# Weight differences of a Strassen output projection: own buffers and later stores for the second half, GpSimd alone for the first half

## The chip, the cores and the metric

The kernel runs on one core of one Trainium2 chip. The metric is the device time of one execution in microseconds (us); of several runs the median counts.

## What is computed

One decoder layer on 512 positions of width 2048, in float32. From the reference, cut to what matters here:

```python
mod = cond @ w_ada[l] + b_ada[l]
shift, scale, gate = jnp.split(mod, 3, axis=-1)
h = rms_norm(x, norm_g[l]) * (1.0 + scale[:, None, :]) + shift[:, None, :]
z = h @ w_in[l]
u_a, v_a, g_a, q_b, k_b, v_b, g_b, f_b = jnp.split(z, pts, axis=-1)
y_a = chunked_spatial_gating(gelu(u_a), gelu(v_a), ...) * silu(g_a)
y_b = forgetting_attention(q_b, k_b, v_b, f_b, b_f[l]) * silu(g_b)
y = jnp.concatenate([y_a, y_b], axis=-1) @ w_out[l]
x = x + gate[:, None, :] * y
return rms_norm(x, final_g)
```

## The kernel before, in words

Every float32 operand of a product is split into a high and a low part, and each product is made of three matmuls on TensorE: high by high, high by low, low by high. A weight tile is loaded into a ring of four buffers (tag `raw`), ScalarE writes the high part (`whi`, line 129) and VectorE the low part (`wlo`, line 130), both in rings of two (`w_tile`, lines 117 to 131). So a tile is split while TensorE works on the tile before it.

The stages follow each other in this order: the conditioning and `h`; the columns `u` and most of the gate of group A (tiles `st`); `v` of group A (`va`, 16 weight tiles); the rest of the gate (`ga`); then four passes of attention, each for four of the 16 heads: the columns `q`, `k`, `vb` and the gate `gb`; last the output projection.

Attention is woven into these products. After each weight tile `tick` (line 133) takes one entry of `slots` (attention, lines 468 to 565) and one of `fillers`. In a pass the scores are made first (lines 484 to 491), then `lse` (line 495) takes their logarithm, transposes it and splits it into `lt`, and eight small copies (line 507) carry `lt` into the rows of the `q` tiles that the second score products (lines 523 and 524, tile `t`) read.

The output projection is one level of a Strassen scheme. It needs four differences of the blocks of `w_out` for each half `u` of the columns. They are made early, beside other products, and kept in device memory (`tsum`): a step loads four blocks into one buffer, subtracts in place, and stores the result. For the first half this is `sum_step` (line 613), woven between the tiles of `va`, eight steps; the buffers are those of tags `vs` (even steps) and `pth`, `ptl` (odd steps), and the four subtractions of line 628 go in turn to GpSimd and VectorE. For the second half it is `sum_part` (line 635), sixteen pieces `ts{k}_{p}` half as wide, all on GpSimd (line 644); each piece takes one buffer of the ring `raw`, is loaded by lines 640 and 641 and stored by line 646. The fillers before them are the gate's steps (`gate_step`, line 594, and `gate_sum`, line 648), which use the ring `raw` too.

SP issues nearly all transfers, in one queue and in order. The order in each engine's queue is set by a scheduler when the program is built, from the order of the code, from priorities (weight tiles are put ahead) and from its own model of times; `tc.issue_after` holds an instruction behind another one.

The tile `wsp` holds the spatial weights of group A until `va` has been mixed; later `wide` (line 1000), scratch of the second output half, takes the same place.

Of the kernel before, what the change touches and what calls it, by code (L numbers as in the profile page):

```python
# [8 lines left out]
F32 = mybir.dt.float32  # L9
F32R = mybir.dt.float32r  # L10
BF16 = mybir.dt.bfloat16
AF = mybir.ActivationFunctionType
ALU = mybir.AluOpType
# [14 lines left out]
def trunk_kernel(  # L28
# [69 lines left out]

    newest = [None]
    newest_mm = [None]  # L100

    def load(dst, src, late=False):
        with ExitStack() as es:
            if queue:
                es.enter_context(tc.issue_after((newest[0] if late else queue[-1]).ins))
            newest[0] = nc.sync.dma_start(dst, src)
            if CHAIN[0]:
                queue.append(newest[0])

    hh = [None] * KB  # L110
    hl = [None] * KB
# [5 lines left out]
    def w_tile(segs, k0, nk, src=win_r, name="", pri=WPRI, loeng=None):  # L117
        n = sum(w for _, w in segs)
        with tc.high_priority(offset=pri):
            raw = wp.tile([P, nk, n], F32, tag="raw", name=f"raw_{name}", bufs=4)  # L120
            o = 0
            for c0, w in segs:
                (load if pri == 0 else nc.sync.dma_start)(
                    raw[:, :, o : o + w], src[:, k0 : k0 + nk, c0 : c0 + w]
                )
                o += w
            hi = wp.tile([P, nk, n], F32R, tag="whi", name=f"whi_{name}")
            lo = wp.tile([P, nk, n], F32R, tag="wlo", name=f"wlo_{name}")
            nc.scalar.activation(hi, raw, AF.Copy)  # L129
            (loeng or nc.vector).tensor_tensor(lo, raw, hi.bitcast(F32), ALU.subtract)  # L130
        return hi, lo
# [292 lines left out]

    fsplit = pb.tile([16, 2, S], F32R, name="fsplit", tag="fs")
    vs_ = []
    wsp = pb.tile([P, 8, 2, P], F32R, name="wsp", tag="wsp")
    OFF = [0, 512, 896, 1152]
    sgb = {}

# [182 lines left out]
    def sum_step(u, k):  # L613

        js = slice((k % 2) * 512, (k % 2) * 512 + 512)
        w = wout_r[:, :, u * 1024 : (u + 1) * 1024].rearrange("p k (s n) -> p k s n", s=2)
        if k % 2:
            a = [pb.tile([P, 2, 512], F32, tag=t, name=f"ts{t}{u}_{k}") for t in ("pth", "ptl")]
        else:
            o = pb.tile([P, 4, 512], F32, tag="vs", name=f"ts{u}_{k}")  # L620
            a = [o[:, 0:2, :], o[:, 2:4, :]]
        nc.sync.dma_start(a[0], w[:, 8 + k])
        nc.sync.dma_start(a[1], w[:, k])
        b11, b12, b21, b22 = (a[z // 2][:, z % 2, :] for z in range(4))
        for z, (dst, l, r) in enumerate((
            (b11, b12, b11), (b12, b12, b22), (b22, b22, b11), (b21, b21, b22),
        )):
            (nc.vector if z % 2 else nc.gpsimd).tensor_tensor(dst, l, r, ALU.subtract)
        if k % 2:
            nc.sync.dma_start(tsum[u][k // 2][:, 0:2, js], a[0])  # L630
            nc.sync.dma_start(tsum[u][k // 2][:, 2:4, js], a[1])
        else:
            nc.sync.dma_start(tsum[u][k // 2][:, :, js], o)

    def sum_part(u, k, p):

        c = slice(p * 256, p * 256 + 256)
        a = wp.tile([P, 4, 256], F32, tag="raw", name=f"ts{u}_{k}_{p}", bufs=4)
        w = wout_r[:, :, u * 1024 : (u + 1) * 1024].rearrange("p k (s n) -> p k s n", s=2)
        nc.sync.dma_start(a[:, 0:2, :], w[:, 8 + k, :, c])  # L640
        nc.sync.dma_start(a[:, 2:4, :], w[:, k, :, c])
        b11, b12, b21, b22 = (a[:, z, :] for z in range(4))
        for dst, l, r in ((b11, b12, b11), (b12, b12, b22), (b22, b22, b11), (b21, b21, b22)):
            nc.gpsimd.tensor_tensor(dst, l, r, ALU.subtract)  # L644
        o = (k % 2) * 512 + p * 256
        nc.sync.dma_start(tsum[u][k // 2][:, :, o : o + 256], a)

    def gate_sum(g):
        gsl = slice(2 * D + g * 512, 2 * D + (g + 1) * 512)
        bg = wp.tile([P, 512], F32, name=f"bg{g}", tag="raw", bufs=4)  # L650
        nc.sync.dma_start(bg, b_ada[:, gsl].broadcast_to([P, 512]))
        gp = bank("x", f"gp{g}")
        nc.tensor.matmul(gp, ones, gate[:, g, :], start=True, stop=True)
        nc.vector.tensor_tensor(gate[:, g, :], gp, bg, ALU.add)
# [4 lines left out]
    def spatial_weights():  # L659
        ws = wp.tile([P, 8, P], F32, tag="raw", name="ws", bufs=4)  # L660
        load(ws, w_s[0].rearrange("h t s -> t h s"), late=True)
        load(
            bias2.rearrange("p h t -> p (h t)"),
            b_s.rearrange("a h t -> a (h t)").broadcast_to([P, 8 * P]), late=True,
        )
        nc.gpsimd.affine_select(
            out=ws, in_=ws, pattern=[[0, 8], [-1, P]], compare_op=ALU.is_ge,
            fill=0.0, base=0, channel_multiplier=1,
        )
        for i in range(2):  # L670
            wt = bank("x", f"wsT{i}")
            for j in range(4):
                nc.tensor.transpose(wt[:, j * P : (j + 1) * P], ws[:, 4 * i + j, :], ident)
            wt32 = pb.tile([P, 512], F32, name=f"wt32_{i}", tag="p", bufs=2)
            nc.scalar.activation(wt32, wt, AF.Copy)
            split(
                wsp[:, 4 * i : 4 * i + 4, 0, :], wsp[:, 4 * i : 4 * i + 4, 1, :],
                wt32.rearrange("p (h t) -> p h t", t=P),
            )
            rp = bank("x", f"rsw{i}")  # L680
            nc.tensor.matmul(rp, ones, wt32, start=True, stop=True)
            for j in range(4):
                h = 4 * i + j
                nc.vector.scalar_tensor_tensor(
                    bias2[:, h, :], rp[:, j * P : (j + 1) * P], lngb[:, 8 + h : 9 + h],
                    bias2[:, h, :], ALU.mult, ALU.add,
                )
# [71 lines left out]
    def mix_head(h):  # L759
# [2 lines left out]
        js = slice(j * P, (j + 1) * P)  # L762
        mt = pb.tile([P, 512], F32, name=f"mt{h}", tag="p", bufs=2)
        b2 = bias2[:, h, :]
        w2 = wsp[:, h].rearrange("p a t -> p (a t)")
        for n in range(2):
            mx = bank("x", f"mix{h}_{n}")
            for i in range(2):
# [28 lines left out]
    vs_.append(pb.tile([P, NT, 4, P], F32R, name="vs", tag="vs"))  # L797
    v_group(0)
    heads_tiles()
    for g in range(4):  # L800
        for i in range(8):
            fillers.append(lambda g=g, i=i: gate_step(g, i))
            if g and i == 2:
                fillers.append(lambda g=g: gate_sum(g - 1))
    parts = [lambda k=k, p=p: sum_part(1, k, p) for k in range(8) for p in range(2)]
    fillers.extend(parts[:3] + [lambda: gate_sum(3)] + parts[3:])
    qk_group(0)
    g_group(0)
    for u in range(1, 4):
# [153 lines left out]
    def unit(u):  # L963
# [33 lines left out]
        X = [bank("x", f"woX{u}_{t}") for t in range(2)]  # L997
        product(X, "S2", w_sum(3, "p6"), True)
        if u:
            wide = pb.tile([P, 4, 512], F32, name="wide", tag="wsp")  # L1000
            u2, u3 = [wide[:, t, :] for t in range(2)], [wide[:, 2 + t, :] for t in range(2)]
        else:
            u2, u3 = tiles("u2", "yb", 8), tiles("u3", "yb", 8)
        evac(lambda t: nc.vector.tensor_tensor(u2[t], X[t], c1[t], ALU.add))
# [123 lines left out]
```

## Time and profile before

| | us |
|---|---|
| median of 3 runs (911.5 to 913.87) | 913.16 |
| the profiled execution: its own time | 910.78 |
| its span, first to last instruction | 909.1 |
| TensorE busy | 880.1 (97%) |
| VectorE busy | 603.9 (66%) |
| ScalarE busy | 445.4 (49%) |
| GpSimd busy | 405.9 (45%) |

The profile is of one execution. Matmuls are pipelined, so a busy TensorE can still lose time: the granted clock of a window says at what share of full speed it ran. A wait is named by what ended last before the instruction could start.

### The profile page before, as it was taken

The numbers are of one execution on the slowest core, as the hardware profiler recorded it, in microseconds if no ns is written. First come the engines' busy times: TensorE is split into PE (matmuls) and PEld (weight loads), VectorE is DVE, ScalarE is ACT, GpSimd is POOL, SyncE is SP. The second block draws the span as 40 slices with busy tenths as digits, with TensorE's granted clock in tenths as the row PEclk, the third lists the DMA queues.
The fourth block names the chain that finished last, engine by engine and source line by source line (L and its number), as shares of the span: only waits on it lengthen the run. The fifth ranks groups of instructions, "written<-read, shape, count | busy, mean of one in ns | idle before, by whom it ended". The sixth has DMA issues, their size and how long they took to land.

```text
span 909.1 us, 12698 instructions
## 1 busy us (share of the span) xinstructions
PE 880.1 (97%) x4408; PEld 744.3 (82%) x4408; DVE 603.9 (66%) x998; ACT 445.4 (49%) x775; POOL 405.9 (45%) x322
## 2 busy tenths in 40 slices
PE   6999999999999999999999999989999999999995
PEld 4888888887878997777889888978898888888884
DVE  4778888374547857454886554535655679996687
ACT  5663323452313234455666544645556657655454
POOL 1356554513324259888988879334641000000001
PEclk8999999999999999999999999999999999999999
DMA  9999996349893264545545454657686236577575
GB/s 339 353 352 355 355 318 202 110 147 323 305 332 110 51 190 140 154 144 156 170 129 163 152 148 155 201 182 220 208 246 203 76 104 220 186 242 250 180 238 202
DMA packets 139713, 188.91 MB, mean 208 GB/s; under 512 B 9968, under 2 KB 103360, under 8 KB 139136
## 3 DMA queue, kind: packets, MB, share of 16 engines
q1 hardware_dynamic: 139216, 187.53, 64.6%
q8 instruction: 35, 0.57, 0.3%
q10 hardware_dynamic: 432, 0.57, 0.2%
q14 instruction: 30, 0.25, 0.1%
HBM read 166.90 MB, written 20.97 MB: 207 GB/s over the span
## 4 chain that ended last, share of the span: by engine, by line
PE 77%; DMA 10%; DVE 5%; POOL 3%; issue 2%; ACT 2%; SPq 0%; POOLq 0%; ACTq 0%; DVEq 0%
PE s L145 6%; PE s L147 6%; PE s L146 6%; PE va L156 3%; PE va L155 3%; PE va L154 3%; PE gb L145 3%; PE gb L146 3%; PE gb L147 3%; PE vb L154 3%; PE vb L156 3%; PE vb L155 3%; PE k L147 2%; PE k L146 2%; PE woZ L911 2%
## 5 line engine op out<-in xcount | busy, mean ns | idle before, releaser
L603 POOL TENSOR_SCALAR gate<-gate,sc 128x512 f32<-128x512 f32 x60 | 103.7, 1738 | 24.5 <-DMA gate<-in_w_ada_dram 11.9
L604 POOL TENSOR_TENSOR gate<-gate,gate 128x512 f32<-128x512 f32 x60 | 92.0, 1536 | 1.7
L130 POOL TENSOR_TENSOR wlo_st<-raw_st,whi_st 128x1024 fp32r<-128x1024 f32 (+3 forms) x36 | 68.4, 1904 | 54.1 <-ACT whi_st L129 52.9
L145 PE MATMUL s<-hh,whi_st 128*128 128x512 f32 x224 | 87.8, 395 | 1.5 <-ACT hh L267 1.5
L146 PE MATMUL s<-hl,whi_st 128*128 128x512 f32 x224 | 87.8, 392 | 0.0
L66 ACT ACTIVATE whi_p<-p 128x1024 fp32r<-128x1024 f32 x52 | 55.2, 1061 | 55.2 <-PE woZ L912 20.1
L644 POOL TENSOR_TENSOR ts<-ts 128x256 f32<-128x256 f32 x64 | 53.3, 837 | 62.8 <-DMA ts<-in_w_out_dram 43.8
L244 DVE SCALAR_TENSOR_TENSOR acc<-ada,sc,acc 128x512 f32<-128x512 f32 x98 | 73.9, 754 | 6.7 <-DMA ada<-in_w_ada_dram 4.0
L67 DVE TENSOR_TENSOR wlo_p<-p,whi_p 128x1024 fp32r<-128x1024 f32 x52 | 63.4, 1220 | 20.2 <-ACT whi_p L66 20.1
L147 PE MATMUL s<-hh,wlo_st 128*128 128x512 f32 x224 | 76.1, 393 | 0.0
L155 PE MATMUL vb<-whi_vb,hl 128*128 128x256 f32 (+1 forms) x256 | 72.6, 286 | 0.0
L154 PE MATMUL vb<-whi_vb,hh 128*128 128x256 f32 (+1 forms) x256 | 71.8, 284 | 0.0
L156 PE MATMUL vb<-wlo_vb,hh 128*128 128x256 f32 (+1 forms) x256 | 71.1, 286 | 0.0
L129 ACT ACTIVATE whi_st<-raw_st 128x1024 fp32r<-128x1024 f32 (+3 forms) x36 | 31.2, 870 | 66.7 <-PE s L146 38.8
L955 POOL TENSOR_TENSOR sfin<-sfin,nhalf 128x1 f32<-128x1 f32 x2 | 1.5, 749 | 137.4 <-DVE sfin L1047 137.4
L145 PE MATMUL q<-hh,whi_q 128*128 128x512 f32 x128 | 51.4, 401 | 1.2 <-ACT whi_q L129 1.2
L146 PE MATMUL q<-hl,whi_q 128*128 128x512 f32 x128 | 51.0, 398 | 0.0
L145 PE MATMUL gb<-hh,whi_gb 128*128 128x512 f32 x128 | 50.4, 393 | 0.5 <-ACT whi_gb L129 0.5
L145 PEld LDWEIGHTS s<-hh,whi_st 128*128 128x128 f32 x224 | 42.4, 190 | 10.3 <-ACT hh L267 1.6
L145 PE MATMUL k<-hh,whi_k 128*128 128x512 f32 x128 | 50.0, 391 | 0.7 <-ACT whi_k L129 0.7
L154 PE MATMUL va<-whi_va,hh 128*128 128x512 f32 x128 | 50.3, 393 | 0.0
L147 PE MATMUL q<-hh,wlo_q 128*128 128x512 f32 x128 | 50.2, 399 | 0.1
(309 smaller groups left out, 2506.3 us busy)
## 6 DMA issues: line engine op xcount, KB each, us to landing
ada<-in_w_ada_dram SPq DMA_DIRECT2D x128, 256.0 KB
gate<-in_w_ada_dram SPq DMA_DIRECT2D x32, 512.0 KB
p<-ts SPq DMA_DIRECT2D x32, 512.0 KB
p<-in_w_out_dram SPq DMA_DIRECT2D x24, 512.0 KB
raw_va<-in_w_in_dram SPq DMA_DIRECT2D x16, 512.0 KB
raw_q<-in_w_in_dram SPq DMA_DIRECT2D x16, 512.0 KB
raw_k<-in_w_in_dram SPq DMA_DIRECT2D x16, 512.0 KB
raw_gb<-in_w_in_dram SPq DMA_DIRECT2D x16, 512.0 KB
```

The lines of the kernel that those rows point to most:

```text
L66: a = nc.scalar.activation(hi, src, AF.Copy)
L67: return a, (eng or nc.vector).tensor_tensor(lo, src, hi.bitcast(F32), ALU.subtract)
L130: (loeng or nc.vector).tensor_tensor(lo, raw, hi.bitcast(F32), ALU.subtract)
L145: nc.tensor.matmul(pt, hi[:, j, cs], hh[k], start=(k == first), stop=False)
L146: nc.tensor.matmul(pt, hi[:, j, cs], hl[k], start=False, stop=False)
L147: nc.tensor.matmul(pt, lo[:, j, cs], hh[k], start=False, stop=(k == last))
L154: nc.tensor.matmul(o, ah[k][:, tsl], hi[:, j, :], start=(k == first), stop=False)
L155: nc.tensor.matmul(o, al[k][:, tsl], hi[:, j, :], start=False, stop=False)
L156: nc.tensor.matmul(o, ah[k][:, tsl], lo[:, j, :], start=False, stop=(k == last))
L244: nc.vector.scalar_tensor_tensor(sb if kk == KB - 1 else a, ga[:, j], col, a, ALU.mult, ALU.add)
L603: nc.gpsimd.tensor_scalar(ga[:, j], ga[:, j], sc[:, kk : kk + 1], None, ALU.mult)
L604: nc.gpsimd.tensor_tensor(a, a, ga[:, j], ALU.add)
```

## The change

It has three parts. In `sum_step` all four subtractions go to GpSimd. In `sum_part` the buffer is no longer one of the ring `raw` but one of two of the tag `wsp`; `wsp` and `wide` become two tiles each for that. The loads and the store of a piece are held behind the newest load of a weight tile (`newest_w`), and a store is put off until the next piece begins. The fillers come in the order: all steps of the gate, two empty entries, the gate's last sum, then the sixteen pieces, then the last store.

```diff
@@ w_tile
-                (load if pri == 0 else nc.sync.dma_start)(
+                newest_w[0] = (load if pri == 0 else nc.sync.dma_start)(
                     raw[:, :, o : o + w], src[:, k0 : k0 + nk, c0 : c0 + w]
                 )
@@
-    wsp = pb.tile([P, 8, 2, P], F32R, name="wsp", tag="wsp")
+    wsp = [pb.tile([P, 4, 2, P], F32R, name=f"wsp{i}", tag="wsp", bufs=2) for i in range(2)]
@@ sum_step
-            (nc.vector if z % 2 else nc.gpsimd).tensor_tensor(dst, l, r, ALU.subtract)
+            nc.gpsimd.tensor_tensor(dst, l, r, ALU.subtract)
@@ sum_part
+    late_stores = []
+
     def sum_part(u, k, p):
 
         c = slice(p * 256, p * 256 + 256)
-        a = wp.tile([P, 4, 256], F32, tag="raw", name=f"ts{u}_{k}_{p}", bufs=4)
+        while late_stores:
+            late_stores.pop(0)()
+        a = pb.tile([P, 4, 256], F32, tag="wsp", name=f"ts{u}_{k}_{p}", bufs=2)
         w = wout_r[:, :, u * 1024 : (u + 1) * 1024].rearrange("p k (s n) -> p k s n", s=2)
-        nc.sync.dma_start(a[:, 0:2, :], w[:, 8 + k, :, c])
-        nc.sync.dma_start(a[:, 2:4, :], w[:, k, :, c])
+        for z, row in ((0, 8 + k), (2, k)):
+            with tc.issue_after(newest_w[0].ins):
+                nc.sync.dma_start(a[:, z : z + 2, :], w[:, row, :, c])
...
-        nc.sync.dma_start(tsum[u][k // 2][:, :, o : o + 256], a)
+
+        def store():
+            with tc.issue_after(newest_w[0].ins):
+                nc.sync.dma_start(tsum[u][k // 2][:, :, o : o + 256], a)
+
+        late_stores.append(store)
@@ fillers
-    fillers.extend(parts[:3] + [lambda: gate_sum(3)] + parts[3:])
+    gates.extend([lambda: None] * 2 + [lambda: gate_sum(3)])
...
+    while gates or parts:
+        if gates:
+            fillers.append(gates.pop(0))
...
+        else:
+            fillers.append(parts.pop(0))
...
+    fillers.append(lambda: [f() for f in late_stores])
@@ unit
-            wide = pb.tile([P, 4, 512], F32, name="wide", tag="wsp")
-            u2, u3 = [wide[:, t, :] for t in range(2)], [wide[:, 2 + t, :] for t in range(2)]
+            wide = [pb.tile([P, 2, 512], F32, name=f"wide{t}", tag="wsp", bufs=2) for t in range(2)]
+            u2, u3 = [w[:, 0, :] for w in wide], [w[:, 1, :] for w in wide]
```

The lines of the changed kernel are two further on at the places below (`sum_part`: 648 for both loads, 656 for the store), and the order of the queues is another. Three places of it follow.

VectorE, late in the `va` stage: `wlo_va_8` to `wlo_va_14` are the low parts of weight tiles, `ts_6`, `tspth_7` and `tsptl_7` buffers of two steps of the first half. Before:

```order
L130 TENSOR_TENSOR wlo_va_8_2334<-raw_va_8_2331,whi_va_8_2333 128x1024
L628 TENSOR_TENSOR ts_6_2391<-ts_6_2391 128x512 x2
L130 TENSOR_TENSOR wlo_va_10_2364<-raw_va_10_2361,whi_va_10_2363 128x1024
L628 TENSOR_TENSOR tspth_7_2459<-tspth_7_2459,tsptl_7_2460 128x512
L628 TENSOR_TENSOR tsptl_7_2460<-tsptl_7_2460 128x512
L130 TENSOR_TENSOR wlo_va_12_2402<-raw_va_12_2399,whi_va_12_2401 128x1024
L130 TENSOR_TENSOR wlo_va_14_2432<-raw_va_14_2429,whi_va_14_2431 128x1024
```

Now, on the same engine at the same place:

```order
L132 TENSOR_TENSOR wlo_va_4_2265<-raw_va_4_2262,whi_va_4_2264 128x1024
L132 TENSOR_TENSOR wlo_va_6_2295<-raw_va_6_2292,whi_va_6_2294 128x1024
L132 TENSOR_TENSOR wlo_va_8_2335<-raw_va_8_2332,whi_va_8_2334 128x1024
L132 TENSOR_TENSOR wlo_va_10_2365<-raw_va_10_2362,whi_va_10_2364 128x1024
L132 TENSOR_TENSOR wlo_va_12_2403<-raw_va_12_2400,whi_va_12_2402 128x1024
L132 TENSOR_TENSOR wlo_va_14_2433<-raw_va_14_2430,whi_va_14_2432 128x1024
```

The subtractions are gone from this queue and stand in GpSimd's, four of a step behind each other.

SP, around the copies of `lt` in the third pass (`u` = 2; the weights `q_0` to `q_12` and `k_0` are those of the fourth pass). `ts_1_1`, `ts_2_0` and `ts_2_1` are pieces of the second half; `raw_...` are loads of weight tiles. Before:

```order
L123 DMA raw_q_0_5636<-in_w_in_dram 128x4x256
L646 DMA ts_0_1850<-ts_1_1_5610 512x1x256
L640 DMA ts_2_0_5714<-in_w_out_dram 128x2x256
L641 DMA ts_2_0_5714<-in_w_out_dram 128x2x256
L123 DMA raw_q_4_5722<-in_w_in_dram 128x4x256
L646 DMA ts_1_1851<-ts_2_0_5714 512x1x256
L640 DMA ts_2_1_5799<-in_w_out_dram 128x2x256
L123 DMA raw_q_8_5807<-in_w_in_dram 128x4x256
L641 DMA ts_2_1_5799<-in_w_out_dram 128x2x256
L507 DMA q_1_3069<-lt_5506 1x4x128 x2
```

Now, on SP:

```order
L656 DMA ts_0_1851<-ts_1_0_5699 512x1x256
L648 DMA ts_1_1_5784<-in_w_out_dram 128x2x256 x2
L125 DMA raw_q_8_5791<-in_w_in_dram 128x4x256
L648 DMA ts_2_0_5870<-in_w_out_dram 128x2x256 x2
L656 DMA ts_0_1851<-ts_1_1_5784 512x1x256
L125 DMA raw_q_12_5877<-in_w_in_dram 128x4x256
L648 DMA ts_2_1_5921<-in_w_out_dram 128x2x256
L656 DMA ts_1_1852<-ts_2_0_5870 512x1x256
L648 DMA ts_2_1_5921<-in_w_out_dram 128x2x256
L125 DMA raw_k_0_5946<-in_w_in_dram 128x4x256
L509 DMA q_1_3070<-lt_5488 1x4x128 x2
```

The same pieces stand ahead of the copies as before, and two more weight loads; the store of a piece stands behind the loads of the next one.

TensorE, at the end of `vb_12` of the third pass and the start of `q_0`: `lse` is the transpose, `gp` the gate's last product, `t` the second scores. Before:

```order
L154 MATMUL vb_3_5241<-whi_vb_12_5524,hh_1638 128x256
L500 MATMUL lse_5504<-ident,nm_5296 16x128
L653 MATMUL gp_5519<-gate,ones 128x512
L155 MATMUL vb_3_5241<-whi_vb_12_5524,hl_1639 128x256
L156 MATMUL vb_3_5241<-wlo_vb_12_5525,hh_1638 128x256
L523 MATMUL t_0_5578<-q_0_3068,k_0_3076 128x512
```

Now `lse` stands in the middle of `vb_12`, and `gp` in the tile before:

```order
L158 MATMUL vb_1_5232<-wlo_vb_12_5509,hh_1633 128x256
L502 MATMUL lse_5486<-ident,nm_5289 16x128
L156 MATMUL vb_1_5232<-whi_vb_12_5508,hh_1638 128x256
L157 MATMUL vb_1_5232<-whi_vb_12_5508,hl_1639 128x256
L158 MATMUL vb_1_5232<-wlo_vb_12_5509,hh_1638 128x256
```

Twenty-seven products of `vb_12` follow the transpose now, two did before. The products of line 524, which need the copies, came behind 21 products of `q_0`; now (line 526) they come behind 25.

## Rows read from the trace of the kernel before

**Rows 1.** The page, part 1: busy us (share) and instructions of TensorE

```profile
PE 880.1 (97%) x4408; PEld 744.3 (82%) x4408; DVE 603.9 (66%) x998; ACT 445.4 (49%) x775; POOL 405.9 (45%) x322
```

**Rows 2.** What TensorE waits for: us in total, times, longest

```profile
PE t L524 <- DMA q<-lt: 3.8, 1, 3.8
...
PE va L156 <- DVE wlo_va L130: 1.3, 1, 1.3
...
PE s L484 <- ACT s L490: 1.2, 2, 1.0
```

**Rows 3.** Windows: us, busy (count) of PE, PEld, DVE, ACT, POOL; clock, DMA share, GB/s

```profile
265.00:270.00 5.00, 3.73 (x17) 2.77 (x16) 3.60 (x4) 0.74 (x1) 2.42 (x2) 1.00 1.01 331
...
608.75:612.57 3.82, 0.00 (x1) 0.03 (x1) 0.00 (x0) 0.00 (x0) 0.72 (x1) 0.79 0.76 234
612.57:618.00 5.43, 5.43 (x14) 4.43 (x15) 2.90 (x7) 2.99 (x6) 2.71 (x4) 0.52 0.32 94
...
681.00:683.00 2.00, 1.00 (x9) 0.80 (x8) 0.82 (x1) 1.91 (x6) 1.30 (x3) 1.00 0.59 205
```

**Rows 4.** The chain of waits from 596 to 613: start, us, what

```profile
602.86 0.75 POOL ts L644
603.62 3.18 DMA ts<-ts
...
608.30 0.71 SPq L507
609.05 3.39 DMA q<-lt
```

**Rows 5.** Timeline of VectorE in the third pass: start, us, what [idle before]

```profile
564.31 1.80 DVE L130 TENSOR_TENSOR wlo_k<-raw_k,whi_k 128x1024 fp32r<-128x1024 f32 x1 [4.21 <-ACT whi_k L129]
...
586.11 1.22 DVE L130 TENSOR_TENSOR wlo_vb<-raw_vb,whi_vb 128x1024 fp32r<-128x1024 f32 x1
...
599.60 0.18 DVE L498 TENSOR_TENSOR nm<-nm,rs 128x16 f32<-128x16 f32 x1 [0.30 <-ACT rs L497]
...
602.52 0.28 DVE L67 TENSOR_TENSOR lt<-lse,lt 16x128 fp32r<-16x128 f32 x1 [0.37 <-ACT lt L66]
```

**Rows 6.** Timeline of VectorE in the `va` stage

```profile
262.20 0.69 DVE L628 TENSOR_TENSOR ts<-ts 128x512 f32<-128x512 f32 x1 [6.08 <-DMA ts<-in_w_out_dram]
...
264.90 2.32 DVE L130 TENSOR_TENSOR wlo_va<-raw_va,whi_va 128x1024 fp32r<-128x1024 f32 x1
```

**Rows 7.** Timeline of ScalarE in the `va` stage

```profile
259.24 1.06 ACT L129 ACTIVATE whi_va<-raw_va 128x1024 fp32r<-128x1024 f32 x1 [4.38 <-PE va L155]
...
277.13 1.06 ACT L129 ACTIVATE whi_ga<-raw_ga 128x1024 fp32r<-128x1024 f32 x1 [4.38 <-PE va L155]
```

**Rows 8.** Timeline of GpSimd in the `va` stage, first and last subtraction of one pair

```profile
205.47 1.28 POOL L628 TENSOR_TENSOR ts<-ts 128x512 f32<-128x512 f32 x1 [20.70 <-DMA ts<-in_w_out_dram]
...
212.69 2.21 POOL L628 TENSOR_TENSOR tsptl<-tsptl,tspth 128x512 f32<-128x512 f32 x1 [1.83 <-DVE tspth L628]
```

**Rows 9.** Timeline of SP: the load of `raw_ga_0`

```profile
258.32 0.66 SPq L123 DMA_DIRECT2D raw_ga<-in_w_in_dram  x1
```

**Rows 10.** The chain of waits from 596 to 685: long landings

```profile
630.04 5.66 DMA ts<-in_w_out_dram
...
671.08 6.11 DMA ts<-ts
677.21 3.80 DMA raw_vb<-in_w_in_dram
```

**Rows 11.** Timeline of TensorE at the `lse` transpose

```profile
601.79 0.28 PE L154 MATMUL vb<-whi_vb,hh 128*128 128x256 f32 x1
601.91 0.27 PE L500 MATMUL lse<-ident,nm 128*16 128x128 f32 x1
```

**Rows 12.** Timeline of SP: the copies of `lt` in the fourth pass

```profile
693.35 6.29 SPq L507 DMA_DIRECT2D q<-lt  x8
```

**Rows 13.** The chain of waits, the fourth pass's second scores

```profile
699.84 0.57 PE t L524 x4
```

More of the change, by code (lines that the diff above doesn't have):

```diff
@@ L100, in trunk_kernel @@
     newest_mm = [None]
+    newest_w = [None]
     def load(dst, src, late=False):
@@ L108, in load @@
                 queue.append(newest[0])
+        return newest[0]
     hh = [None] * KB
@@ L676, in spatial_weights @@
             split(
-                wsp[:, 4 * i : 4 * i + 4, 0, :], wsp[:, 4 * i : 4 * i + 4, 1, :],
+                wsp[i][:, :, 0, :], wsp[i][:, :, 1, :],
                 wt32.rearrange("p (h t) -> p h t", t=P),
@@ L764, in mix_head @@
         b2 = bias2[:, h, :]
-        w2 = wsp[:, h].rearrange("p a t -> p (a t)")
+        w2 = wsp[h // 4][:, h % 4].rearrange("p a t -> p (a t)")
         for n in range(2):
@@ L799, in trunk_kernel @@
     heads_tiles()
+    gates = []
     for g in range(4):
         for i in range(8):
-            fillers.append(lambda g=g, i=i: gate_step(g, i))
+            gates.append(lambda g=g, i=i: gate_step(g, i))
             if g and i == 2:
-                fillers.append(lambda g=g: gate_sum(g - 1))
+                gates.append(lambda g=g: gate_sum(g - 1))
+    gates.extend([lambda: None] * 2 + [lambda: gate_sum(3)])
     parts = [lambda k=k, p=p: sum_part(1, k, p) for k in range(8) for p in range(2)]
-    fillers.extend(parts[:3] + [lambda: gate_sum(3)] + parts[3:])
+    n = 0
+    while gates or parts:
+        if gates:
+            fillers.append(gates.pop(0))
+        elif False:
+            fillers.append(lambda: None)
+        else:
+            fillers.append(parts.pop(0))
+        n += 1
+    fillers.append(lambda: [f() for f in late_stores])
     qk_group(0)
```

## The prediction

> **What bounds the kernel now.** I read the shares of the engines first. TensorE (PE) is busy 97% of the span [rows 1], so a change can win only where PE stands still or runs slowly. Next I read the list of what PE waits for. Outside the start and the end of the program three waits are over a microsecond and lie where the diff works: the score products of the third pass (line 524) wait 3.8 us for the small copies `q<-lt`, a `va` product waits 1.3 us for the split on VectorE (DVE), and a score product waits 1.0 us for ScalarE (ACT) [rows 2]. Then I cut windows around them [rows 3]: PE does nothing for 3.82 us before 612.57, and in the 5.43 us behind it the granted clock is 0.52, half speed, 1.2 GHz; the two shorter gaps, 1.27 us at 265 and 1.0 us at 681, leave it at 1.00. Last I followed the chain of waits back from 612.57 [rows 4]. GpSimd (POOL) finishes a piece of weight differences at 603.6, its store takes 3.18 us to land, then SP, which issues almost every transfer and in order, comes to the copies of line 507 at 608.30. They land, and PE starts 4.27 us after that issue. What they copy (`lt`) had been split at 602.80 [rows 5]. So SP's queue, not a product, costs this place its time.
>
> **The change, part by part** (line numbers of before).
>
> *First half on POOL alone (line 628).* Sixteen subtractions leave DVE and go to POOL. DVE is not the bound; what counts is the order in it. The split `wlo_va_10` stood behind two subtractions. DVE sat idle 6.08 us for their transfer, subtracted at 262.20, waited for POOL again and began the split at 264.90 [rows 6], though ACT had begun its half of it at 259.24 [rows 7]. In the new order nothing of line 628 stands in DVE, so the split follows ACT's 1.06 us at once and the 1.27 us of PE go: **minus 1.27**. The price is on POOL: a pair of steps takes 205.47 to 214.90, 9.4 us, now [rows 8] and will take eight times 1.28, 10.3 us. Both engines can also block each other. One POOL subtraction took 2.21 us instead of 1.28 beside a split, and the split of 264.90 took 2.32 us [rows 6, 8].
>
> The Trainium skill (SBUF — State Buffer, Who interferes with whom) says that a DVE instruction with two SBUF inputs contends with a GpSimd instruction that reads SBUF, and that the loser blocks wholly; the 2.21 and 2.32 us agree. If every split of the stage met such a block, the sum below would be 902.8, and if none did, 902.1.
>
> If each of the four splits in a pair hits one subtraction at +0.93, a pair takes 14.0 us, 4.6 more than now. Three pairs stand on SP ahead of the next weights, `raw_ga_0`: it was issued at 258.32 [rows 9] and is needed at 277.13 [rows 7]. Even with 5.66 us to land (the slowest load among my rows [rows 10]) 13.1 us are spare, against 3 x 4.6 = 13.8. So this costs 0, at worst 0.7. A split that loses once ends 1.06 + 1.28 + 1.22 = 3.6 us after ACT begins it, and ACT begins the next after 4.38 + 1.06 = 5.4 us [rows 7]: nothing.
>
> *Own buffers for the second half.* Its pieces no longer take slots of the four-deep ring `raw`, so a weight load waits only for splits of weights and gates, no longer for a store to land. In the new order `raw_q_12` and `raw_k_0` stand ahead of the copies of line 507; before, they stood behind. The late wait at 681 came from there: a store took 6.11 us to land, the weights behind it another 3.80 [rows 10], and ACT held that split ahead of the scores. With two more weight loads ahead of the same products, this goes: **minus 1.0**.
>
> *Later stores.* A store now goes out beside the next piece's loads, behind a weight load. This adds waits: with two buffers a load waits until the store of the piece two earlier has landed, and behind it on SP stand `raw_q_12`, `raw_k_0` and the copies of line 507. I follow that chain. `raw_q_4` waits for `wlo_vb_8`, done at 587.33 [rows 5]. From there to the first copy stand nine issues of some 0.5 us (an estimate; the copies take 0.79 each [rows 12]), one load to land (L), four subtractions of 0.75 [rows 4] and one store to land (S): 587.33 + 4.5 + 3.0 + L + S. With L = 5.66 and S = 3.18 [rows 4, 10], a slow load and an ordinary store, it is 603.7, and PE could go on 4.27 later, at 607.9. When does PE come there? It came at 608.75 after 21 products of `q`; now 25 stand ahead, four more at 0.24 (twice the 0.12 of a product of half the columns [rows 11]), so 609.7. The wait vanishes with 1.8 us to spare: **minus 3.82**, and with no idle stretch the slow clock goes too, 5.43 x (1 - 0.52) = **minus 2.6**. At the other end, S = 6.11 and issues of 0.79, the copies go at 609.2, PE could go on at 613.5 and waits 3.8 us, with the clock 6.4: all of this gain is gone. I take the first value since it already holds the slowest load.
>
> *The `lse` transpose* moves up by 25 products of 0.12 us, from 601.91 [rows 11] to 598.9, and to 599.4 with the gate's product put ahead. Its operand `nm` was written at 599.60 [rows 5] behind ACT's 1 us for `whi_q_0`, which now comes after it. So PE waits 0, at most 0.4.
>
> *The rest.* The pieces start three steps later and end two later; nothing reads them before the second output half. `wide` in two tiles and `wsp` in two tiles hold the same bytes. POOL's memsets for the last pass (line 454) stand behind pieces as before, and by the chain above the pieces in front of them load no later. Nothing, both ways.
>
> **Sum**, against the profiled execution of 910.78: 3.82 + 2.6 + 1.0 + 1.27 = 8.7, so 902.1. The median of the three runs stands 2.38 above that execution; on its scale I forecast **904.5 us**.
>
> **The rivals.**
>
> *A: the copies still come late.* They remain behind two pieces on SP, and the new loads wait for stores. For it: landings of 5.66 and 6.11 us occur in this very stretch. Against: both must meet in one chain. Then only the two short gaps are won, 904.5 + 6.4 = 910.9.
>
> *B: two buffers are too few, and it ends slower.* A buffer's cycle is L + S + 3.0 and three issues, 1.5; a piece takes half. The first can load once `wlo_k_12` is done, 566.1 [rows 5], plus an issue. The sixteenth then needs its load, 6.7, its subtractions, 3.0, its store and two weight issues ahead of the last pass's copies, 1.5, and 4.27 to reach PE: 566.6 + 15 P + 15.5. PE came to that place at 699.84 [rows 13], with the copies issued at 693.35 [rows 12]; by my sum it comes 8.7 earlier, at 691.1. So P above 7.3 us decides. With 5.66 and 3.18 P is 6.7, with 5.66 and 6.11 it is 8.1: then PE is held until 703.6, 12.5 us, plus 2.6 of slow clock: 919.6. Against it: it needs sixteen slow landings in a row, where the rows have them singly.
>
> *C: POOL is the bound of the first half.* Sixteen subtractions at 1.28 instead of 0.69 [rows 6, 8] are 9.4 us more, and if they all ended on the way of the weights the time would be 913.9. The spare 13.1 us of `raw_ga_0` speak against it.
>
> The Trainium skill (GPSIMD Engine Reference, Engine selection) sends elementwise work on two inputs to VectorE, since GpSimd is about twice slower. The two durations agree, 1.28 to 0.69.
>
> *D: part of the gain is taken back* by a wait in the new order, such as `lse` or a score bank: 2 to 3 us, 907.
>
> **How the numbers follow.** A measurement of this kernel tells about 0.3%, 2.7 us, from no change. Forecast 0.72, D 0.05: faster, 0.77. A 0.12 and C 0.03 lie within the 2.7 us: same, 0.15. B 0.08: slower. The range reaches from 901.5, three microseconds under the forecast for the spread of the runs (2.4) and small gaps that close too, to 911.5, which takes in A; B and C are left out.
>
> **What would show it.** Right: no wait of line 524 on `q<-lt` in the third pass, granted clock 1.00 around 610, the first copy issued before 605; no `va` product waiting for DVE; the weights of `q` and `k` issued some 10 us earlier than now. Wrong: SP waiting for stores ahead of the copies (A, B), or `raw_va` and `raw_ga` landing after they are needed with POOL busy throughout (C).

## The result and the profile after

| us | before | changed |
|---|---|---|
| median | 913.5 (8 runs, 911.5 to 921.45) | 905.82 (8 runs, 903.15 to 909.44) |
| ratio, 95% interval | | 0.9908 [0.9878, 0.9937] |
| profiled execution | 910.78 | 907.83 |
| its span | 909.1 | 906.1 |

The forecast was 904.5. The changed kernel is 7.7 us faster, by 0.9%, and the interval of the ratio lies wholly below 1.

The two profiled executions differ by 3.0 us only. Part of this lies in the first 40 us, where both kernels have the same code but the clock rises at different times: the granted clock of 0 to 40 us is 0.87 in the execution before and 0.74 in this one, and the first product of `s` (line 145 before, 147 now) begins at 30.48 and at 33.05. Two executions of the kernel before differ by 9 us at this place (30.48 and, in e11 below, 39.79), so traces are compared below from that product to the end of the span: before 909.1 - 30.48 = **878.62**, changed 906.1 - 33.05 = **873.05**. The medians probably hold such executions too: of the 64 runs of the kernel before in the groups below, 15 lie between 918 and 925 with a granted clock over the whole run near the 0.973 of e11, and without them its medians are 912.7 to 913.1.

The page, part 1, of the changed kernel answers to [rows 1]:

```profile
PE 880.7 (97%) x4408; PEld 745.3 (82%) x4408; DVE 593.8 (66%) x982; ACT 445.5 (49%) x775; POOL 436.9 (48%) x338
```

TensorE's work is the same; sixteen instructions have gone from DVE to POOL. What TensorE waits for, against [rows 2]:

```profile
PE t L526 <- DMA q<-lt: 2.3, 2, 2.1
...
PE s L486 <- ACT s L492: 0.2, 1, 0.2
```

The wait of `va` for DVE is gone, the wait at the scores fell from 1.2 to 0.2, and line 526 waits 2.3 us in two parts instead of 3.8 in one. Windows, the first four at or near the cuts of [rows 3]:

```profile
265.00:270.00 5.00, 5.00 (x24) 4.14 (x23) 1.54 (x1) 1.06 (x1) 3.03 (x3) 1.00 0.98 361
608.00:611.60 3.60, 3.57 (x16) 2.63 (x14) 0.28 (x1) 0.39 (x1) 0.98 (x2) 1.00 0.74 230
611.78:618.00 6.22, 6.21 (x29) 5.22 (x30) 4.39 (x9) 5.25 (x11) 2.30 (x4) 1.00 0.57 165
681.00:683.00 2.00, 2.00 (x19) 2.00 (x18) 0.76 (x2) 1.14 (x3) 0.00 (x0) 1.00 0.74 240
694.20:696.60 2.40, 0.34 (x2) 0.00 (x0) 0.00 (x0) 2.08 (x2) 0.00 (x0) 1.00 0.52 181
696.60:702.00 5.40, 5.35 (x25) 4.51 (x26) 3.81 (x9) 3.19 (x8) 0.00 (x0) 1.00 0.58 165
```

In the third pass PE is busy at full clock, but for the 0.2 us between the second window and the third. The larger part of the 2.3 us lies in a new place: 2.1 us in the **fourth** pass, after which the clock stays at 1.00. SP in the third pass, against [rows 4] (start, us, what; a gap between two lines that follow each other is SP standing still):

```profile
591.54 0.53 SPq L656 DMA_DIRECT2D ts<-ts  x1
...
600.63 0.52 SPq L656 DMA_DIRECT2D ts<-ts  x1
...
604.14 0.37 SPq L648 DMA_DIRECT2D ts<-in_w_out_dram  x1
605.04 0.53 SPq L656 DMA_DIRECT2D ts<-ts  x1
605.62 0.69 SPq L648 DMA_DIRECT2D ts<-in_w_out_dram  x1
606.40 0.93 SPq L125 DMA_DIRECT2D raw_k<-in_w_in_dram  x1
607.38 5.90 SPq L509 DMA_DIRECT2D q<-lt  x8
```

The load at 604.14 waited for the store of 600.63 to land, 3.5 us, as the prediction's chain has it. The store at 591.54 waited for GpSimd, which had subtracted from 588.78 to 591.51. TensorE needed the copies at 611.57 and went on at 611.78: it did not wait long, but nothing was to spare. SP in the fourth pass, against [rows 12]:

```profile
680.94 1.65 SPq L648 DMA_DIRECT2D ts<-in_w_out_dram  x2
...
688.86 0.52 SPq L656 DMA_DIRECT2D ts<-ts  x1
689.44 1.72 SPq L125 DMA_DIRECT2D raw_gb<-in_w_in_dram  x2
691.26 6.06 SPq L509 DMA_DIRECT2D q<-lt  x8
```

and what it waited for, on GpSimd, and when `lt` was ready, on VectorE:

```profile
686.46 2.38 POOL L651 TENSOR_TENSOR ts<-ts 128x256 f32<-128x256 f32 x3 [0.70 <-DMA ts<-in_w_out_dram]
...
688.06 0.28 DVE L67 TENSOR_TENSOR lt<-lse,lt 16x128 fp32r<-16x128 f32 x1 [0.37 <-ACT lt L66]
```

SP stands from 683.2, behind a weight load, to 688.86 at the last piece's store, until its subtractions end at 688.84. Two weight loads follow, and the copies of `lt`, which was ready at 688.34, leave at 691.26.

The first half's pair of steps on GpSimd, first and last subtraction, against [rows 8]:

```profile
208.19 1.28 POOL L630 TENSOR_TENSOR ts<-ts 128x512 f32<-128x512 f32 x1 [20.90 <-DMA ts<-in_w_out_dram]
...
219.53 2.34 POOL L630 TENSOR_TENSOR tsptl<-tsptl 128x512 f32<-128x512 f32 x1
```

A pair takes 13.7 us, 9.4 before. SP issues `raw_ga_0` later, 266.16 for 258.32, and ScalarE needs it at nearly the same time [rows 7, 9]:

```profile
266.16 0.39 SPq L125 DMA_DIRECT2D raw_ga<-in_w_in_dram  x1
...
278.24 1.06 ACT L131 ACTIVATE whi_ga<-raw_ga 128x1024 fp32r<-128x1024 f32 x1 [4.38 <-PE va L157]
```

### The profile page after: what moved, and what is told of

Same layout as the page of the kernel before. It is cut to its first block, busy times and chain, and to the rows that moved or that the text cites. A ratio compares the mean times of both kernels' runs of the same rounds, so it can differ in the third digit from the quotient of the medians.

```text
span 906.1 us, 12687 instructions
## 1 busy us (share of the span) xinstructions
PE 880.7 (97%) x4408; PEld 745.3 (82%) x4408; DVE 593.8 (66%) x982; ACT 445.5 (49%) x775; POOL 436.9 (48%) x338
## 4 chain that ended last, share of the span: by engine, by line
PE 85%; DMA 5%; DVE 4%; issue 2%; ACT 2%; POOL 1%; SPq 0%; POOLq 0%; ACTq 0%; DVEq 0%
PE s L147 6%; PE s L149 6%; PE s L148 6%; PE vb L156 3%; PE vb L157 3%; PE vb L158 3%; PE va L158 3%; PE va L157 3%; PE va L156 3%; PE gb L149 3%; PE gb L148 3%; PE gb L147 3%; PE q L149 3%; PE q L148 3%; PE k L149 3%; PE q L147 3%
## 5 line engine op out<-in xcount | busy, mean ns | idle before, releaser
L605 POOL TENSOR_SCALAR gate<-gate,sc 128x512 f32<-128x512 f32 x60 | 106.4, 1784 | 23.9 <-DMA gate<-in_w_ada_dram 14.9
L148 PE MATMUL gb<-hl,whi_gb 128*128 128x512 f32 x128 | 50.2, 392 | 0.0
```

Source lines behind the costliest of these rows:

```text
L148: nc.tensor.matmul(pt, hi[:, j, cs], hl[k], start=False, stop=False)
L605: nc.gpsimd.tensor_scalar(ga[:, j], ga[:, j], sc[:, kk : kk + 1], None, ALU.mult)
```

## The experiments

Each run was profiled once. The ratios are to the kernel before in the same group of runs; its medians there were 913.24 (e1 to e4), 913.72 (e5 to e8) and 914.51 (e9 to e12). "From `s` on" is the span less the start of the first product of `s`, both from the kernel's own trace. Line 526 is line 524 in before, e1 and e11.

| kernel | median | ratio, 95% interval | span, first `s` | from `s` on | wait of line 526: third, fourth pass |
|---|---|---|---|---|---|
| before | 913.5 | | 909.1, 30.48 | 878.6 | 3.8, 0 |
| e11: before again | 922.36, one run | | 920.6, 39.79 | 880.8 | 4.4, 0 |
| changed | 905.82 | 0.9908 [0.9878, 0.9937] | 906.1, 33.05 | 873.1 | 0.2, 2.1 |
| e10: changed again | 905.74 | 0.9895 [0.9861, 0.9928] | 907.2, 33.08 | 874.1 | 0.8, 0 |
| e1: only GpSimd alone | 913.04 | 1.0006 [0.9972, 1.004] | 914.1, 33.1 | 881.0 | 3.2, 0 |
| e2: all but GpSimd alone | 905.24 | 0.9919 [0.9887, 0.9951] | 903.7, 30.4 | 873.3 | 1.0, 1.4 |
| e3: ring `raw` | 921.84 | 1.0098 [1.0062, 1.0135] | 927.2, 39.1 | 888.1 | 11.3 in two, the longer in the fourth |
| e4: no hold | 952.97 | 1.0449 [1.0405, 1.0493] | 958.2, 39.5 | 918.7 | none over 0.7 |
| e5: last store later | 905.3 | 0.9918 [0.989, 0.9946] | 902.2, 30.8 | 871.4 | 1.0, 0 |
| e6: pieces two steps earlier | 909.8 | 0.9957 [0.9923, 0.9991] | 910.1, 32.9 | 877.2 | 2.8, 0 |
| e7: store at once | 910.1 | 0.9992 [0.9962, 1.0022] | 906.7, 33.05 | 873.7 | 3.0, 0 |
| e8: old order | 909.18 | 0.9948 [0.9929, 0.9968] | 910.7, 31.3 | 879.4 | 4.6, 0 |
| e9: one gap, last store later | 902.41 | 0.9866 [0.9821, 0.991] | 899.9, 31.36 | 868.5 | 0, 0 |
| e12: more work on GpSimd | 905.06 | 0.9895 [0.9834, 0.9956] | 903.1, 30.4 | 872.7 | 0.9, 0 |

### Is the first half worth its stall? (e1, e2, e11)

e1 is the kernel before with the first half's edit alone; e2 is the changed kernel without it:

```diff
-            (nc.vector if z % 2 else nc.gpsimd).tensor_tensor(dst, l, r, ALU.subtract)
+            nc.gpsimd.tensor_tensor(dst, l, r, ALU.subtract)
```

> The kernel before with one edit: all four subtractions of line 628 on GpSimd. Theory (the first half is worth its one stall): the va product's 1.27 us wait at 265 goes, the third pass keeps its 3.8 us wait on the copies and the half clock behind it, so the time is 1.3 us below before, 0.9986 of it, less than the measurement can tell; in its profile the row of va waiting for DVE is gone and a pair of steps on GpSimd takes 12 to 14 us instead of 9.4. Rival (first half gives nothing, or costs): another va wait of over 1 us appears, on ACT, DVE or a late weight tile, and the time is equal or above. Second rival (the first half gives much of the 7.7 us): 3 us or more below before.

> The changed kernel with the first half's subtractions on GpSimd and VectorE in turn, as before. Theory (terms add up): the va wait of about 1.3 us near 265 is back and nothing else moves, so 1.3 us above the changed kernel, about 907; the third pass still shows no wait of over 1 us on the copies. Rival (the first half on GpSimd costs as much as it gives, since its pairs took 13.6 us): equal to the changed kernel or 1 us below it.

e1 loses the `va` wait and is not faster: 1.0006. e2 has no `va` wait either, although the split there stands behind the same two subtractions as before, and is as fast as the changed kernel. e11 asks the kernel before a second time:

> The kernel before itself, for a second profile. Theory (the va product's wait of 1.3 us near 265 is one execution's chance, since it went too when the subtractions alternated as before): under 0.5 us there, while the 3 to 4 us wait on the copies of the third pass and the half clock behind it are seen again. Rival (it belongs to the order of VectorE's queue): 1 us or more again.

What its TensorE waits for:

```profile
PE t L524 <- DMA q<-lt: 4.4, 1, 4.4
...
PE s L484 <- ACT s L490: 1.3, 2, 1.1
```

The wait on the copies and that at the scores are there again, with the clock at 0.57 over the 5.7 us behind the copies; the list has no row of `va`. The split of `wlo_va_10` [rows 6] and the product that needs it, now in e11:

```profile
273.98 1.22 DVE L130 TENSOR_TENSOR wlo_va<-raw_va,whi_va 128x1024 fp32r<-128x1024 f32 x1
...
275.73 0.39 PE L156 MATMUL va<-wlo_va,hh 128*128 128x512 f32 x1
```

The split begins 4.85 us after ScalarE's half of it (269.13) and ends 0.5 us before TensorE needs it. In e2 it begins 3.65 us behind that half, in the first profile of before 5.66, where it also lost against a subtraction on GpSimd and took 2.32 us instead of 1.22 [rows 6, 7]. So the old order brings the split close to being late, but the wait came in one of the three executions that have it. The theory of e2 falls, and its rival holds; that of e1, a gain too small for its times, loses its ground, since the wait is no fixed part of the kernel before. **The edit of the first half is worth nothing that these runs can tell**, and they show no cost.

### Which part of the second half carries the gain? (e3, e4, e7, e8)

The label above each edit names the run.

```diff
 e3
-        a = pb.tile([P, 4, 256], F32, tag="wsp", name=f"ts{u}_{k}_{p}", bufs=2)
+        a = wp.tile([P, 4, 256], F32, tag="raw", name=f"ts{u}_{k}_{p}", bufs=4)
 e4 (both places)
-            with tc.issue_after(newest_w[0].ins):
+            if True:
```

> The changed kernel, but the pieces of the second half take slots of the ring raw again (later stores, the issue order held behind weight loads and the order of the fillers stay). Theory A (the queue: what counts is what stands on SP ahead of the copies and when it is free): the copies of the third pass now stand behind the load of ts_2_0, which needs a slot of the ring that the store of an earlier piece frees; with stores put off by one piece the ring holds two pieces and two weights, so loads come later: a wait of 2 to 6 us in the third pass with half clock behind it, 909 to 915. Theory B (own buffers do nothing, later stores and the order do all): no such wait, within 1 us of the changed kernel.

> The changed kernel without the two holds behind the newest weight load. The pieces move up: on SP all sixteen now stand ahead of the third pass, among the loads of the gate. Theory A (the queue): with no piece ahead of the copies in the third and the fourth pass, both their waits go, the 2.1 us of the fourth pass too, and the time is 2 us below the changed kernel, about 904, provided the first two passes stay without new waits. Rival (the pieces cost the same wherever they stand): they now delay the gate's loads and the weights of the first two passes, with waits of 2 us or more there, and the time is equal to or above the changed kernel.

e3: theory B falls. A had the cause right and the place wrong: the third pass shows hardly a wait, the fourth 11 us. The chain of waits of e3 into that place:

```profile
691.05 3.81 DMA ts<-ts
...
695.30 3.38 DMA ts<-in_w_out_dram
...
708.02 3.50 DMA ts<-ts
...
712.00 0.69 SPq L509
```

With the ring, loads and stores of pieces follow each other on SP one landing at a time, 3.4 to 3.8 us each, and the copies leave at 712.00. This is the mechanism of rival B of the prediction, too few buffers, in a kernel whose pieces share four buffers with the weights; that its 921.84 is near the 919.6 of the rival, which was priced for two own buffers, tells nothing. **Own buffers** are worth 888.1 - 873.1 = 15 us beside the other parts of the change. They are not worth that alone: the kernel before has the ring too and takes 878.6, so with the ring the other parts cost 9.5 us.

e4: the copies are never late, as theory A wanted, and yet it is the slowest kernel of all; the rival holds. Its largest wait is on a split of weights, 11.6 us in seven parts:

```profile
PE k L147 <- ACT whi_k L131: 11.6, 7, 2.7
```

and the windows of the first two passes, e4

```profile
340.00:600.00 260.00, 229.16 (x1080) 184.00 (x1079) 131.97 (x225) 118.43 (x240) 222.75 (x173) 0.96 0.58 183
```

and the changed kernel:

```profile
340.00:600.00 260.00, 255.85 (x1337) 216.93 (x1336) 152.15 (x266) 141.58 (x285) 214.39 (x146) 1.00 0.52 161
```

GpSimd is busy for over 80% of the time there in both kernels, in the changed one with the gate. In e4 the pieces' subtractions and loads stand among those of the gate, on GpSimd and on SP, the weights come late, PE has 26.7 us less busy time in 260, and its clock is 0.96 on average. So the pieces need **the hold** to stay out of these passes.

```diff
 e7
-        late_stores.append(store)
+        store()
 e8
-    gates.extend([lambda: None] * 2 + [lambda: gate_sum(3)])
...
+    gates = gates + parts[:3] + [lambda: gate_sum(3)]
+    parts = parts[3:]
```

> The changed kernel, but each store is issued in the code right behind its piece's subtractions and not when the next piece begins. Theory (own buffers carry the gain; putting the store off moves only one place of SP's queue): the third pass is as in the changed kernel, with at most 1 us of wait, the fourth pass keeps its 2.1 us, 905 to 907. Rival (the later stores carry the gain, since SP no longer waits there for GpSimd): SP waits at each store, the copies of the third pass come 3 us later or more, the 3.8 us wait and the half clock are back: 911 or more.

> The changed kernel with the order of the fillers of before: three pieces ahead of the gate's last sum, no empty fillers. Theory (the third pass has no reserve): the load of ts_3_1, which needs a buffer that a store must leave first, stands right ahead of the copies of the third pass, so they go out 3 to 4 us later than in the changed kernel; a wait of 3 to 4 us with half clock behind it, less the 2.1 us of the fourth pass: 908 to 910. Rival (the order of the fillers does not matter, own buffers and later stores do): 904 to 906.

e8 agrees with its theory: a wait of 4.6 us in the third pass with half the clock behind it, none in the fourth, 909.18. **The order of the fillers** is a part of the gain; the trace shows it more clearly than the times, whose intervals touch ([0.9929, 0.9968] and [0.9878, 0.9937]).

e7 stays open. Its median, 910.1, is near the rival's, and its third pass does wait 3.0 us with a lower clock behind it (0.50 from 614 to 616):

```profile
609.60:612.80 3.20, 0.20 (x1) 0.00 (x0) 0.00 (x0) 2.34 (x2) 1.43 (x3) 1.00 0.72 230
...
612.84:618.00 5.16, 5.16 (x17) 4.27 (x18) 3.91 (x9) 3.19 (x8) 1.32 (x3) 0.67 0.58 170
```

But its copies on SP,

```profile
608.49 5.22 SPq L509 DMA_DIRECT2D q<-lt  x8
```

left only 1.1 us after those of the changed kernel, with the same start of `s`, 33.05; TensorE was there 1.8 us earlier (612.84 less the wait of 3.04, against 611.57), and line 526 went on at 612.84 against 611.78. From `raw_q_8` to the copies the two traces have the same order on SP. The edit moved one store in the code, and what it changed here is one exchange further ahead: the store of 590.17 stands in front of `raw_q_4`, that of 591.54 in the changed kernel behind it. From `s` on the two traces are 0.6 us apart; the medians are 4.3 apart, with four of the twelve runs above 915, and the ratio in the table, 0.9992, is not that of the medians (0.996). So this run does not test the rival, a queue that stands at every store. **What the later stores are worth alone is not shown.**

### The fourth pass (e5, e6, e10)

```diff
 e5
-    fillers.append(lambda: [f() for f in late_stores])
+    fillers.extend([lambda: None] * 3 + [lambda: [f() for f in late_stores]])
 e6
-    gates.extend([lambda: None] * 2 + [lambda: gate_sum(3)])
+    gates.extend([lambda: gate_sum(3)])
```

> The changed kernel with the very last store three fillers later, so that on SP it stands behind the copies of the fourth pass; nothing else moves. Theory (SP waits at that store, for GpSimd, from 683 to 689, while lt is ready at 688.3): the copies go out at about 688.5 instead of 691.3, land by 693.7, before TensorE comes at 694.5; the 2.1 us wait of line 526 is gone and the time is 2 us below the changed kernel, 0.9885 of before, about 903.7. Rival (the copies are held by something else, such as a weight load behind VectorE, or land late anyway): the wait stays at 1 us or more.

> The changed kernel without the two empty fillers, so every piece stands two weight tiles earlier. Theory (pieces are paced by the weights they are held behind): the last store is off the fourth pass's copies, whose 2.1 us wait goes, and the third pass stays without a wait: about 903.7. Rival (pieces are paced by their two buffers, and the third pass has no reserve): on SP one more store and load, of ts_3_0 and ts_3_1, stand ahead of the third pass's copies; they go out 3 to 4 us later, TensorE waits about as long and its clock falls to half behind it: 5 us up, less the 2.1, 908 to 909.

SP of e5:

```profile
679.26 3.34 SPq L125 DMA_DIRECT2D raw_gb<-in_w_in_dram  x3
685.41 5.32 SPq L509 DMA_DIRECT2D q<-lt  x8
```

The copies no longer stand behind the store, and leave while VectorE still splits `lt` (685.42 to 685.70); in the changed kernel they left 2.9 us behind the split. The cause named for the 2.1 us is right. The median gains 0.5 us only, which the intervals cannot tell from none.

> The changed kernel itself, for a second profile and for times beside the run above. Theory (the third pass has no reserve): line 526 waits between 0 and 1.5 us in the third pass, as in the runs that share this order, and 1.5 to 2.5 us in the fourth; the time is again 905 to 906. Rival (the wait of the fourth pass is one execution's chance): under 0.5 us there.

The same kernel again has no wait in the fourth pass and 0.8 us in the third. The rival was right on the first, the theory on the second and on the time. But what is missing is the wait, not the loss:

```profile
689.29 0.53 SPq L656 DMA_DIRECT2D ts<-ts  x1
...
691.69 6.29 SPq L509 DMA_DIRECT2D q<-lt  x8
```

```profile
697.39 0.74 PE L526 MATMUL t<-q,k 128*128 128x512 f32 x4
```

SP stood at the same store until 689.29, and the copies left no earlier than the 691.26 of the first profile. TensorE came to line 526 at 697.39 instead of 694.54. It was 2.3 us behind already in the third pass, chiefly by a wait of 1.4 us for VectorE at 458 with a clock of 0.69 over 5.5 us behind it. How long the traces take from `s` to line 526:

| us | before | e11 | changed | e10 | e2 | e12 | e7 | e5 | e9 |
|---|---|---|---|---|---|---|---|---|---|
| third pass | 582.1 | 583.5 | 578.7 | 581.0 | 579.3 | 579.9 | 579.8 | 578.4 | 576.4 |
| fourth pass | 669.2 | 671.5 | 663.6 | 664.3 | 663.5 | 663.3 | 664.2 | 661.0 | 659.1 |

Behind the fourth pass all nine take another 209.3 to 210.5 us. The five traces with the last store ahead of the copies come to line 526 of the fourth pass within 1.1 us of each other, though they are up to 2.3 apart in the third pass. e5, with the store behind them, is 2.3 us and more ahead of all five. Its median does not show as much, which stays open.

e6 follows its rival: the copies of the third pass leave at 611.71, and TensorE waits 2.8 us. So the third pass has no reserve in the changed kernel, and one piece, two loads and a store, on SP decides it. The last of them in e6:

```profile
608.77 1.00 SPq L648 DMA_DIRECT2D ts<-in_w_out_dram  x2
610.42 0.52 SPq L656 DMA_DIRECT2D ts<-ts  x1
...
611.71 1.60 SPq L509 DMA_DIRECT2D q<-lt  x2
```

### A version with reserve at both places (e9)

```diff
+    parts[4:4] = [lambda: None] * 1
...
-    fillers.append(lambda: [f() for f in late_stores])
+    fillers.extend([lambda: None] * 2 + [lambda: [f() for f in late_stores]])
```

> The changed kernel with one empty filler ahead of piece ts_2_0 and the last store two fillers later. On SP one store and one load fewer stand between raw_q_12 and the third pass's copies, and the last store stands behind the fourth pass's copies. Theory (both places are decided by what SP holds ahead of the copies): the third pass's copies go out 3 us or more before those of the changed kernel, relative to when TensorE comes there, no wait of line 526 on the copies in either pass, 2 to 3 us below the changed kernel run beside it. Rival (a piece put off meets another place): a wait of over 1 us appears elsewhere in the third or fourth pass, equal to the changed kernel or slower.

SP and TensorE in its third pass:

```profile
600.10 6.50 SPq L509 DMA_DIRECT2D q<-lt  x8
```

```profile
607.72 0.68 PE L526 MATMUL t<-q,k 128*128 128x512 f32 x3
```

and the windows around line 526 in both passes:

```profile
604.00:611.00 7.00, 7.00 (x34) 5.80 (x33) 2.92 (x8) 3.51 (x6) 2.74 (x4) 1.00 0.47 139
688.00:696.00 8.00, 8.00 (x39) 6.63 (x38) 3.58 (x8) 5.46 (x10) 1.31 (x2) 1.00 0.53 158
```

The copies leave 7.6 us before they are needed, 4.2 in the changed kernel, and PE stands still in neither pass. From `raw_q_8` to the copies SP takes 8.9 us with one piece between them (e9), 13.5 with two (changed) and 17.7 with three (e6). 902.41 is 3.3 us below the changed kernel run beside it (905.74) and 12.1 below before, the lowest median of all these kernels. The theory holds on both waits. On the time the evidence is weaker: the intervals of the two ratios overlap, [0.9821, 0.991] and [0.9861, 0.9928], but four of the six runs lie below the fastest of the ten beside it, 903.41, and from `s` on the trace is 4.5 and 5.6 us shorter than the two of the changed kernel.

### How much more can GpSimd take? (e12)

```diff
             nc.gpsimd.tensor_tensor(dst, l, r, ALU.subtract)
+            if z % 2:
+                nc.gpsimd.tensor_copy(dst, dst)
```

> The changed kernel with two copies of 128x512 in place added on GpSimd in each step of the first half, behind its second and fourth subtraction, four to a pair of steps. With an estimate of 1.3 us each, from the subtractions' rows, a pair goes from 13.6 to some 19 us. Theory (GpSimd's reserve is what is left of the 13.1 us until raw_ga_0 is needed; the changed kernel used 7.8): three pairs with 5.2 us more exceed it, raw_ga_0 comes late and TensorE waits 5 to 10 us there, 911 to 916. Rival (GpSimd has a whole period of four weight tiles, some 18 us, for each pair, so little of it reaches SP): under 2 us more than the changed kernel.

```profile
206.38 1.27 POOL L630 TENSOR_TENSOR ts<-ts 128x512 f32<-128x512 f32 x1 [20.92 <-DMA ts<-in_w_out_dram]
...
221.54 0.61 POOL L632 COPY tsptl<-tsptl 128x512 f32<-128x512 f32 x1
```

A pair grows from 13.7 to 15.8 us only, since a copy takes 0.61 where 1.3 was estimated, and the build put the load of `raw_ga_0` on SP earlier, at 257.06. No new wait of over 0.4 us appears, 905.06. The time agrees with the rival, but the run does not test the limit.

## Why the prediction was right, and where it was not

The median is 1.3 us from the forecast. The main terms are right in their mechanism; that the total comes so near is partly luck, since one term below was no fixed part of the kernel and one place was missed: the terms that hold, 3.6 + 2.6 + 0.8, less the 2.1 of that place, make 4.9 of the 7.7 us.

**Third pass, minus 3.82 and minus 2.6: right.** The chain that the prediction followed is the one that decides. It forecast the copies at 603.7 and TensorE at 609.7. On that execution's scale (`s` began 2.57 later) this is 606.3 and 612.3; measured were 607.38 and 611.57. The copies were 1.1 us later, TensorE 0.7 earlier, and issue to product took 4.40 instead of 4.27. These use up the 1.8 us that were to spare and leave the 0.2 us of wait. One link was missing: the forecast counts from `raw_q_4`, 589.9 on this scale, but SP then stood at a store until 591.54, for GpSimd. In the traces with the same order 0.2 to 1.0 us of wait stand here, at full clock; in the three of the old second half (before, e1, e11) 3.2 to 4.4, and the clock falls.

**The wait at 681, minus 1.0: right.** It is 0.2 now; e1 and e11 show 1.1 again.

**First half, minus 1.27: wrong.** The failed step is "In the new order nothing of line 628 stands in DVE, so the split follows ACT's 1.06 us at once and the 1.27 us of PE go". They go, but the old order does not always bring them: two of its three executions (e2, e11) have no such wait, and the edit alone changes the time by a ratio of 1.0006. The sum took one execution's wait for the kernel's.

**First half on GpSimd at no cost: right, with less to spare than thought.** A pair took 13.7 us, near the upper bound of 14.0. `raw_ga_0` was issued 12.1 us before ScalarE needed it; with the 5.66 us that were allowed for landing 6.4 of the 13.1 us are left. The Trainium skill (SBUF — State Buffer, Who interferes with whom) says that the port pair the two engines share is an exclusive lock. The subtraction of 2.34 us among those of 1.28 agrees: a split of 1.23 us began on VectorE just before it, at 219.50. The pair's 3.4 us above eight times 1.28 are two such subtractions, a third hit for 0.4, and 0.9 of waiting for a load; the prediction allowed four hits of 0.93. Rival C did not occur: 16 slower subtractions did not reach TensorE.

The Trainium skill (GPSIMD Engine Reference, Engine selection) sends such work to VectorE because GpSimd takes about twice as long. The durations agree, 1.28 us to 0.69 [rows 6, 8]. By e1 and e2 the engine made no difference in time here, since the work lies beside TensorE's on either.

**`lse`: right.** No wait of the transpose is in the list.

**"The rest: nothing, both ways": wrong by up to 2.1 us.** The pieces end two steps later, and with them the last store stands ahead of the fourth pass's copies. The prediction looked at this place only as rival B, with the last piece's chain far too late; it did not look for one store just ahead of the copies. The SP rows and e5 show that store as the cause. e10 shows that no wait needs to appear there: TensorE then comes later, for other reasons, and goes on at line 526 664.3 us after `s` instead of 663.6.

**Sum.** Between the two traces: 3.6 + 2.6 + 0.8 + 1.27 - 2.1 = 6.2 us, and from `s` on they differ by 878.62 - 873.05 = 5.6; the second pair, e11 and e10, by 6.7. The first pair holds the 1.27 us of `va`, which the second has not. The medians differ by 7.7. The 1 to 2 us between traces and medians are not placed. Executions differ by more than that at their start, and by some 2 us in the second pass, at 440 (e11) or at 458 (e1, e6, e10).

**The signs.** They came as named, on that execution's scale: the first copy left at 604.8, before 605, `raw_q_8` 16 us earlier than before, with the clock at 1.00 and no `va` product waiting for VectorE. Only the wait on the copies did not go quite to nothing.

## What to carry to other kernels

Where one queue issues everything in order, list for each small urgent transfer what stands ahead of it and what that waits for; a store is ready only when the last engine has finished, so look that it does not stand ahead of the urgent transfers of the next place either. Own buffers alone are not enough: without the hold behind the weights (e4) the freed work moved to where it cost 46 us, and a reserve of under 2 us in a chain of landings is none. Before a stall of a microsecond is entered as a gain, look whether it is in a second execution; and where a wait is gone, compare when the place was reached, since an engine that comes late does not wait.

## What the runs showed of the hardware

The clock behind a wait. Behind the 2.1 us wait of the changed kernel the granted clock is 1.00 (window from 696.60). Behind the 3.0 us of e7 it is 0.67 over 5.16 us (half speed, 1.2 GHz, and then full, 2.4), behind the 3.8 of before 0.52 over 5.43 [rows 3], and behind the 11 us of e3 it is no worse:

```profile
715.45:721.00 5.55, 5.55 (x17) 4.56 (x18) 3.90 (x9) 3.18 (x8) 0.00 (x0) 0.61 0.46 140
```

The loss behind the wait is 5.16 x 0.33 = 1.7 us (e7), 2.6 (before) and 5.55 x 0.39 = 2.2 (e3): the longest wait does not cost the most. Nor does the length of the one wait decide whether the clock falls at all. In the second pass the first product of `q` waits 2.5 us for ScalarE in e8 and in e11. The windows behind it, e8 and then e11:

```profile
431.24:436.50 5.26, 5.26 (x26) 4.49 (x27) 3.98 (x7) 2.88 (x8) 4.74 (x2) 1.00 0.53 158
```

```profile
440.70:446.00 5.30, 5.29 (x18) 4.42 (x19) 3.98 (x7) 2.92 (x8) 4.71 (x2) 0.70 0.51 169
```

And behind 1.4 us, with another of 0.4 close by, the clock falls in e10:

```profile
459.50:465.00 5.50, 5.50 (x20) 4.42 (x20) 4.23 (x8) 3.31 (x7) 5.50 (x3) 0.69 0.14 48
```
